# Add and GELU on one core: one DMA queue with late stores, adds on GpSimd, a sigmoid form through PSUM

## The chip, the core and the metric

The kernel runs on one core of one Trainium2 chip. The core has five engines that run side by side, each through its own list of instructions in order: TensorE (PE, not used here), VectorE (DVE), ScalarE (ACT), GpSimd (POOL) and SyncE (SP, which here only issues transfers). Sixteen DMA engines carry data between the chip's main memory (HBM) and the on-chip memory SBUF, which has 128 partitions. A second on-chip memory, PSUM, can be read and written by VectorE and ScalarE. The metric is the device time of one execution in microseconds (us); lower is better.

## The reference

Two float32 arrays of 1024 rows and 4096 columns are added, and the tanh form of GELU is taken of the sum, element by element:

```python
def reference(x, y):
    z = x + y
    return (0.5 * z * (1 + np.tanh(np.sqrt(2 / np.pi) * (z + 0.044715 * z ** 3)))).astype(np.float32)
```

Two arrays of 16.8 MB are read and one is written, 50.3 MB in all. Since 0.5 (1 + tanh u) is the sigmoid of 2u, the same function can be written z times sigmoid(2u).

## The kernel before

Each partition owns eight consecutive rows of the arrays, that is 32768 consecutive numbers in HBM. These columns are cut into 15 pieces of 2048 and a tail of 1024, 512, 256, 128 and 128. A piece of 2048 columns is 1 MiB per array: 128 runs of 8 KiB.

For every piece the kernel does eight things:

- two loads, issued by SP (L67 for x into a tile `a`, L68 for y into a tile `b`); six buffers of each;
- on VectorE, z = a + b (L75);
- on ScalarE, w = k3 z squared (the Square at L81, its factor folded into the scale);
- on VectorE, w = (w + k1) z (L90), the argument of tanh;
- on ScalarE, w = tanh(w) (L100), then w = 0.5 w + 0.5 (L105, whose bias is a one-column tile);
- on VectorE, w = z w (L116);
- one store, issued by GpSimd (L117), as soon as the product of the piece is there.

So VectorE has three instructions per piece and ScalarE three. The tiles z and w have five buffers each, all in SBUF. The loop at the end of the function emits the pieces in a software pipeline (loads of piece t beside the add of piece t - 1, and so on), and a scheduler in the tile framework sets the final order on each engine. SP carries loads only: a load of a piece waits until an earlier transfer has landed, and no more than eight loads are in flight. GpSimd carries stores only. The two queues share the sixteen DMA engines.

Of the kernel before, what the change touches and what calls it, by code (L numbers as in the profile page):

```python
# [1 line left out]

# [1 line left out]

# [4 lines left out]


@with_exitstack
def kernel(
    ctx: ExitStack,
    tc: tile.TileContext,
    x: bass.AP,
    y: bass.AP,
    out: bass.AP,
):
    nc = tc.nc  # L20
    P = nc.NUM_PARTITIONS
    fp32 = mybir.dt.float32

    N, D = x.shape
    assert N % P == 0
    rows_per_part = N // P

    k1 = math.sqrt(2.0 / math.pi)
    k3 = k1 * 0.044715
    sqrt_k3 = math.sqrt(k3)  # L30

    xv = x.rearrange("(p n) d -> p (n d)", p=P)
    yv = y.rearrange("(p n) d -> p (n d)", p=P)
    ov = out.rearrange("(p n) d -> p (n d)", p=P)

    total_free = rows_per_part * D
    FMAX = 2048

    tail = [1024, 512, 256, 128, 128]
    nbody = (total_free - sum(tail)) // FMAX  # L40
    assert sum(tail) + nbody * FMAX == total_free
    sizes = [FMAX] * nbody + tail
    offsets = []
    off = 0
    for F in sizes:
        offsets.append(off)
        off += F
    C = len(sizes)

    in_pool = ctx.enter_context(tc.tile_pool(name="inputs", bufs=6))  # L50
    chain_pool = ctx.enter_context(tc.tile_pool(name="chain", bufs=5))
    consts = ctx.enter_context(tc.tile_pool(name="consts", bufs=1))

    half = consts.tile([P, 1], fp32, tag="half")
    nc.vector.memset(half, 0.5)  # L55

    a_t: list = [None] * C
    b_t: list = [None] * C
    z_t: list = [None] * C
    w_t: list = [None] * C  # L60

    def do_load(c):
        F = sizes[c]
        sl = slice(offsets[c], offsets[c] + F)
        a = in_pool.tile([P, F], fp32, tag="a")
        b = in_pool.tile([P, F], fp32, tag="b")
        nc.sync.dma_start(out=a, in_=xv[:, sl])  # L67
        nc.sync.dma_start(out=b, in_=yv[:, sl])  # L68
        a_t[c] = a
        b_t[c] = b  # L70

    def do_add(c):
        F = sizes[c]
        z = chain_pool.tile([P, F], fp32, tag="z")
        nc.vector.tensor_add(out=z, in0=a_t[c], in1=b_t[c])  # L75
        z_t[c] = z

    def do_sq(c):
        F = sizes[c]
        w = chain_pool.tile([P, F], fp32, tag="w")  # L80
        nc.scalar.activation(  # L81
            out=w,
            in_=z_t[c],
            func=mybir.ActivationFunctionType.Square,
            scale=sqrt_k3,
        )
        w_t[c] = w

    def do_stt(c):
        nc.vector.scalar_tensor_tensor(  # L90
            out=w_t[c],
            in0=w_t[c],
            scalar=k1,
            in1=z_t[c],
            op0=mybir.AluOpType.add,
            op1=mybir.AluOpType.mult,
        )

    def do_ti(c):
        nc.scalar.activation(  # L100
            out=w_t[c],
            in_=w_t[c],
            func=mybir.ActivationFunctionType.Tanh,
        )
        nc.scalar.activation(  # L105
            out=w_t[c],
            in_=w_t[c],
            func=mybir.ActivationFunctionType.Identity,
            scale=0.5,
            bias=half,  # L110
        )

    def do_mul_store(c):
        F = sizes[c]
        sl = slice(offsets[c], offsets[c] + F)
        nc.vector.tensor_mul(out=w_t[c], in0=z_t[c], in1=w_t[c])  # L116
        nc.gpsimd.dma_start(out=ov[:, sl], in_=w_t[c])  # L117

    for t in range(C + 4):
        if 0 <= t < C:  # L120
            do_load(t)
        if 0 <= t - 3 < C:
            do_ti(t - 3)
        if 0 <= t - 1 < C:
            do_add(t - 1)
        if 0 <= t - 2 < C:
            do_stt(t - 2)
        if 0 <= t - 1 < C:
            do_sq(t - 1)
        if 0 <= t - 3 < C:  # L130
            do_mul_store(t - 3)


# [1 line left out]
_INS = ['x', 'y']  # L135
_OUTS = [((1024, 4096), 'float32')]


# [23 lines left out]
```

## Time and profile before

| what | value |
|---|---|
| time, median of 3 runs | 132.72 us (132.6 to 132.73) |
| span of the profiled execution, first to last instruction | 130.8 us |
| median less span | 1.9 us |
| VectorE busy | 107.8 us (82% of the span) |
| ScalarE busy | 96.0 us (73%) |
| GpSimd busy | 11.0 us (8%) |
| moved by the loads' queue (q1) and the stores' queue (q0) | 33.56 MB and 16.78 MB |
| mean rate over the span | 385 GB/s |

The profile comes from one execution; the runs of the time table are others. The profiled execution's own time is taken as its span and the 1.9 us that lie around it. The page gives busy times of engines, the traffic of the DMA engines in 40 equal slices of the span (3.27 us each), and the chain of waits that ended last. In the views by window, each row gives a stretch of the span, the busy time of the engines in it, and the DMA engines' rate. SPq and POOLq mark instructions that issue transfers.

### The profile page before, as it was taken

The numbers are of one execution on the slowest core, as the hardware profiler recorded it, in microseconds if no ns is written. First come the engines' busy times: TensorE is split into PE (matmuls) and PEld (weight loads), VectorE is DVE, ScalarE is ACT, GpSimd is POOL, SyncE is SP. The second block draws the span as 40 slices with busy tenths as digits, with TensorE's granted clock in tenths as the row PEclk, the third lists the DMA queues.
The fourth block names the chain that finished last, engine by engine and source line by source line (L and its number), as shares of the span: only waits on it lengthen the run. The fifth ranks groups of instructions, "written<-read, shape, count | busy, mean of one in ns | idle before, by whom it ended". The sixth has DMA issues, their size and how long they took to land.

```text
span 130.8 us, 306 instructions
## 1 busy us (share of the span) xinstructions
DVE 107.8 (82%) x61; ACT 96.0 (73%) x61; POOL 11.0 (8%) x24
## 2 busy tenths in 40 slices
DVE  0053949999999999988959899998969799999930
ACT  3005492899998989895975979885975959899850
POOL 0000002001000000101010100101010100110341
DMA  4999999999999999999999999999999999717690
GB/s 140 428 421 431 431 416 428 341 423 416 439 426 418 436 429 418 436 428 418 436 426 421 436 423 423 434 426 421 436 426 421 417 414 389 310 53 321 271 342 29
DMA packets 8258, 50.35 MB, mean 385 GB/s; under 512 B 960, under 2 KB 1728, under 8 KB 2496
## 3 DMA queue, kind: packets, MB, share of 16 engines
q1 hardware_dynamic: 5760, 33.56, 62.1%
q0 software_dynamic: 2496, 16.78, 30.9%
q14 instruction: 2, 0.02, 0.0%
HBM read 33.55 MB, written 16.78 MB: 385 GB/s over the span
## 4 chain that ended last, share of the span: by engine, by line
DMA 44%; issue 43%; POOL 5%; DVE 3%; POOLq 1%; SPq 0%; DVEq 0%
DMA b<-in_y_dram 44%; POOL out_dram L117 5%; DVE w L90 2%; DVE w L116 2%; POOLq L157 0%; SPq L67 0%; POOLq L117 0%; DVE z L75 0%; DVEq L75 0%
## 5 line engine op out<-in xcount | busy, mean ns | idle before, releaser
L75 DVE TENSOR_TENSOR z<-a,b 128x2048 f32<-128x2048 f32 (+4 forms) x20 | 37.2, 1862 | 13.1 <-DMA b<-in_y_dram 13.1
L81 ACT ACTIVATE w<-z 128x2048 f32<-128x2048 f32 (+4 forms) x20 | 31.3, 1563 | 22.5 <-DVE z L75 22.1
L116 DVE TENSOR_TENSOR w<-z,w 128x2048 f32<-128x2048 f32 (+4 forms) x20 | 37.2, 1860 | 3.0 <-ACT w L105 3.0
L90 DVE SCALAR_TENSOR_TENSOR w<-w,z 128x2048 f32<-128x2048 f32 (+4 forms) x20 | 37.1, 1859 | 2.4 <-ACT w L81 2.4
L100 ACT ACTIVATE w<-w 128x2048 f32<-128x2048 f32 (+4 forms) x20 | 31.3, 1566 | 7.0 <-DVE w L90 6.9
L105 ACT ACTIVATE w<-w,half 128x2048 f32<-128x2048 f32 (+4 forms) x20 | 33.2, 1659 | 0.6
L117 POOL DMA_DIRECT2D out_dram<-w x20 | 10.8, 541 | 116.6 <-DVE w L116 114.7
L81 ACT ACT_TABLE_LOAD x1 | 1.3, 1283 | 0.7 <-PEq L146 0.7
L55 DVE MEMSET half<- 128x1 f32 x1 | 0.1, 59 | 0.8 <-PEq L146 0.8
L146 POOL MEMSET const-float32-0.0<- 128x1 f32 x1 | 0.1, 98 | 0.2 <-issue 0.2
L146 POOL MEMSET const-bfloat16-1.0<- 128x1 bf16 x1 | 0.1, 101 | 0.0
L146 POOL MEMSET const-float32-1.0<- 128x1 f32 x1 | 0.1, 98 | 0.0
L146 POOL MEMSET const-uint8-127<- 128x1 uint8 x1 | 0.1, 98 | 0.0
## 6 DMA issues: line engine op xcount, KB each, us to landing
a<-in_x_dram SPq DMA_DIRECT2D x15, 1024.0 KB, 27.4
b<-in_y_dram SPq DMA_DIRECT2D x15, 1024.0 KB, 28.2
out_dram<-w POOLq DMA_DIRECT2D x15, 1024.0 KB, 9.1
a<-in_x_dram SPq DMA_DIRECT2D x1, 512.0 KB, 28.7
b<-in_y_dram SPq DMA_DIRECT2D x1, 512.0 KB, 26.3
out_dram<-w POOLq DMA_DIRECT2D x1, 512.0 KB, 3.8
a<-in_x_dram SPq DMA_DIRECT2D x1, 256.0 KB, 23.2
b<-in_y_dram SPq DMA_DIRECT2D x1, 256.0 KB, 21.4
```

The costliest lines, as they stand in the source:

```text
L55: nc.vector.memset(half, 0.5)
L75: nc.vector.tensor_add(out=z, in0=a_t[c], in1=b_t[c])
L81: nc.scalar.activation(out=w, in_=z_t[c], func=mybir.ActivationFunctionType.Square, scale=sqrt_k3,)
L90: nc.vector.scalar_tensor_tensor(out=w_t[c], in0=w_t[c], scalar=k1, in1=z_t[c], op0=mybir.AluOpType.add, op1=mybir.AluOpType.mult,)
L100: nc.scalar.activation(out=w_t[c], in_=w_t[c], func=mybir.ActivationFunctionType.Tanh,)
L105: nc.scalar.activation(out=w_t[c], in_=w_t[c], func=mybir.ActivationFunctionType.Identity, scale=0.5, bias=half,)
L116: nc.vector.tensor_mul(out=w_t[c], in0=z_t[c], in1=w_t[c])
L117: nc.gpsimd.dma_start(out=ov[:, sl], in_=w_t[c])
L146: nc = _bacc.Bacc("TRN2", target_bir_lowering=False, num_devices=1)
```

## The change

The kernel function is rewritten. What it computes is the same function in the sigmoid form, and:

- **Pieces.** A tile is now up to 4096 columns of a block of 128 rows: 1024, 1024, 2048, then six of 4096, then 2048, 1024, 512, 512. A transfer of a 4096-column tile is 2 MiB, contiguous in HBM. Compute goes in chunks of up to 1024 columns, 33 of them.
- **x stays.** Every x tile has its own place in SBUF. The sum z is written over x, the product over z, and the store reads from there. y has four buffers of 4096 columns.
- **One queue.** SP issues loads and stores. A store of a tile stands in SP's list where the loads are 8192 columns past the tile's end. Everything left is stored at the end.
- **GpSimd adds.** The add of chunks 2 to 30 (29 of 33) is done by GpSimd; VectorE does the first two and the last two.
- **Sigmoid form, PSUM.** The chunk's temporary w lies in PSUM (four buffers of 1024 columns). ScalarE does a Square and a Sigmoid, VectorE (w + c1) z and w z. The step 0.5 w + 0.5 is gone.
- **Order by hand.** Four lists (SP, GpSimd, ScalarE, VectorE) fix each engine's order. A one-column Sigmoid ahead of everything loads the function table.

The old function is shown whole above, so only the added lines stand here.

```diff
+    c1 = 2.0 * math.sqrt(2.0 / math.pi)
+    root = math.sqrt(c1 * 0.044715)
+    LEAD = 8192
+    CH = 1024
+    YB = 4
+    sizes = [1024, 1024, 2048] + [D] * (NB - 2) + [2048, 1024, 512, 512]
...
+    def hbm(ap, t):
+        n, o = divmod(starts[t], D)
+        assert o + sizes[t] <= D
+        return ap[n * P : (n + 1) * P, o : o + sizes[t]]
...
+    by_pool = set(range(2, C - 2))
+    xpool = ctx.enter_context(tc.tile_pool(name="xz", bufs=1))
+    ypool = ctx.enter_context(tc.tile_pool(name="y", bufs=YB))
+    ppool = ctx.enter_context(
+        tc.tile_pool(name="w", bufs=4, space=bass.MemoryType.PSUM)
+    )
+    def load_x(t):
+        xt[t] = xpool.tile([P, sizes[t]], fp32, tag=f"x{t}", name=f"x{t}")
+        nc.sync.dma_start(out=xt[t], in_=hbm(x, t))
...
+        nc.sync.dma_start(out=yt[t], in_=hbm(y, t))
+    def store(t):
+        nc.sync.dma_start(out=hbm(out, t), in_=xt[t])
...
+    def add(c):
+        t, o, f = chunks[c]
+        eng = nc.gpsimd if c in by_pool else nc.vector
+        eng.tensor_add(out=z(c), in0=z(c), in1=yt[t][:, o : o + f])
+    def sq(c):
+        f = chunks[c][2]
+        wt[c] = ppool.tile([P, CH], fp32, tag="w", name=f"w{c}")[:, :f]
+        nc.scalar.activation(out=wt[c], in_=z(c), func=act.Square, scale=root)
+    def stt(c):
+        nc.vector.scalar_tensor_tensor(
+            out=wt[c], in0=wt[c], scalar=c1, in1=z(c), op0=alu.add, op1=alu.mult
         )
+    def sig(c):
+        nc.scalar.activation(out=wt[c], in_=wt[c], func=act.Sigmoid)
+    def mul(c):
+        nc.vector.tensor_mul(out=z(c), in0=wt[c], in1=z(c))
+    sp, pool, dve, acts = [], [], [], []
+    s = 0
+    for t in range(T):
+        sp += [(load_x, t), (load_y, t)]
+        while s < T and starts[s] + sizes[s] + LEAD <= starts[t] + sizes[t]:
+            sp.append((store, s))
+            s += 1
+    sp += [(store, t) for t in range(s, T)]
...
+    for i in range(-3, C + 1):
+        if 0 <= i < C:
+            dve.append((stt, i))
+            acts.append((sig, i))
+        if 0 <= i - 1 < C:
+            dve.append((mul, i - 1))
+        if 0 <= i + 3 < C and i + 3 not in by_pool:
+            dve.append((add, i + 3))
+        if 0 <= i + 2 < C:
+            acts.append((sq, i + 2))
...
+        one = xpool.tile([P, 1], fp32, tag="one", name="one")
+        nc.vector.memset(one, 0.0)
+        nc.scalar.activation(out=one, in_=one, func=act.Sigmoid)
```

On SP, the list before is loads alone, x and y by turns (`a` and `b` are their tiles):

```order
L67 DMA a<-in_x_dram 128x2048
L68 DMA b<-in_y_dram 128x2048
L67 DMA a<-in_x_dram 128x2048
L68 DMA b<-in_y_dram 128x2048
L67 DMA a<-in_x_dram 128x2048
```

In the new program it stands as below behind the loads of the first three tiles. `x_69`, `x_73` and `x_76` are the first three x tiles, `x_79` and `x_83` the first two of 4096 columns, `y_...` the y tiles.

```order
L74 DMA x_79<-in_x_dram 128x4096
L81 DMA y_81<-in_y_dram 128x4096
L74 DMA x_83<-in_x_dram 128x4096
L81 DMA y_85<-in_y_dram 128x4096
L84 DMA out_dram<-x_69 128x1024
L84 DMA out_dram<-x_73 128x1024
L84 DMA out_dram<-x_76 128x2048
L74 DMA x_127<-in_x_dram 128x4096
L81 DMA y_129<-in_y_dram 128x4096
L84 DMA out_dram<-x_79 128x4096
L74 DMA x_156<-in_x_dram 128x4096
```

The first three stores stand behind the loads of 12 MiB, and from there every store of a full tile stands between the loads of the tile two places on and three places on; those later loads stand behind it.

The end of SP's list in the new program, from the last store that is followed by a load (`x_247`, `x_250` and `x_253` are the small last tiles):

```order
L84 DMA out_dram<-x_156 128x4096
L74 DMA x_243<-in_x_dram 128x2048
L81 DMA y_245<-in_y_dram 128x2048
...
L74 DMA x_253<-in_x_dram 128x512
L81 DMA y_245<-in_y_dram 128x512
L84 DMA out_dram<-x_185 128x4096
L84 DMA out_dram<-x_214 128x4096
L84 DMA out_dram<-x_243 128x2048
L84 DMA out_dram<-x_247 128x1024
L84 DMA out_dram<-x_250 128x512
L84 DMA out_dram<-x_253 128x512
```

Six stores, 6 MiB, now stand behind the last load; before, stores had a queue of their own on GpSimd.

On VectorE, the list before ends like this (L75 is the add, L90 the STT, L116 the product; the pieces shrink):

```order
L75 TENSOR_TENSOR z<-a,b 128x512
L90 SCALAR_TENSOR_TENSOR w<-w,z 128x1024
L75 TENSOR_TENSOR z<-a,b 128x256
L116 TENSOR_TENSOR w<-z,w 128x2048
L90 SCALAR_TENSOR_TENSOR w<-w,z 128x512
L116 TENSOR_TENSOR w<-z,w 128x1024
```

The new program's list at the border to tile `x_79`, and its end (`w_...` are the PSUM temporaries; STT is the SCALAR_TENSOR_TENSOR of the function `stt`, and the TENSOR_TENSOR at L109 is `mul`, at L93 `add`):

```order
L101 SCALAR_TENSOR_TENSOR w_117<-w_117,x_79 128x1024
L109 TENSOR_TENSOR x_76<-w_109,x_76 128x1024
...
L109 TENSOR_TENSOR x_214<-w_287,x_214 128x1024
L93 TENSOR_TENSOR x_250<-x_250,y_245 128x512
L101 SCALAR_TENSOR_TENSOR w_297<-w_297,x_243 128x1024
L109 TENSOR_TENSOR x_243<-w_292,x_243 128x1024
L93 TENSOR_TENSOR x_253<-x_253,y_245 128x512
L101 SCALAR_TENSOR_TENSOR w_303<-w_303,x_247 128x1024
L109 TENSOR_TENSOR x_243<-w_297,x_243 128x1024
L101 SCALAR_TENSOR_TENSOR w_308<-w_308,x_250 128x512
```

The last product of a tile stands behind the first STT of the next tile, and in the end the adds of the last two small tiles stand among the work of `x_243`.

More of the change, by code (lines that the diff above doesn't have):

```diff
@@ L22 @@
     fp32 = mybir.dt.float32
+    act = mybir.ActivationFunctionType
+    alu = mybir.AluOpType
     N, D = x.shape
     assert N % P == 0
[L26 to L85, printed above, removed]
-        )
[L87 to L131, printed above, removed]
+    NB = N // P
+    TOT = NB * D
+    c1 = 2.0 * math.sqrt(2.0 / math.pi)
+    root = math.sqrt(c1 * 0.044715)
+    LEAD = 8192
+    CH = 1024
@@ new lines @@
+    YB = 4
+    sizes = [1024, 1024, 2048] + [D] * (NB - 2) + [2048, 1024, 512, 512]
+    assert sum(sizes) == TOT
+    starts = [sum(sizes[:t]) for t in range(len(sizes))]
+    T = len(sizes)
+    def hbm(ap, t):
+        n, o = divmod(starts[t], D)
+        assert o + sizes[t] <= D
+        return ap[n * P : (n + 1) * P, o : o + sizes[t]]
+    chunks = []
+    for t in range(T):
+        o = 0
+        while o < sizes[t]:
+            f = min(CH, sizes[t] - o)
+            chunks.append((t, o, f))
+            o += f
@@ new lines @@
+    C = len(chunks)
+    last = {t: c for c, (t, _, _) in enumerate(chunks)}
+    by_pool = set(range(2, C - 2))
[4 more added lines that the diff above has]
+    )
+    xt, yb, yt, wt = {}, {}, {}, {}
+    def load_x(t):
+        xt[t] = xpool.tile([P, sizes[t]], fp32, tag=f"x{t}", name=f"x{t}")
+        nc.sync.dma_start(out=xt[t], in_=hbm(x, t))
@@ new lines @@
+    sp, pool, dve, acts = [], [], [], []
+    s = 0
+    for t in range(T):
+        sp += [(load_x, t), (load_y, t)]
[3 more added lines that the diff above has]
+    sp += [(store, t) for t in range(s, T)]
+    for c in range(C):
+        if c in by_pool:
+            pool.append((add, c))
+    for i in range(-3, C + 1):
[8 more added lines that the diff above has]
+            acts.append((sq, i + 2))
@@ new lines @@
+    needs = {
+        load_x: lambda t: [],
+        load_y: lambda t: [
+            (add, c)
+            for c, (i, _, _) in enumerate(chunks)
+            if starts[t] % D == 0 and starts[i] // D == starts[t] // D - YB
+        ],
+        add: lambda c: [(load_y, chunks[c][0]), (load_x, chunks[c][0])],
+        sq: lambda c: [(add, c)] + ([(mul, c - 4)] if c >= 4 else []),
+        stt: lambda c: [(sq, c)],
+        sig: lambda c: [(stt, c)],
+        mul: lambda c: [(sig, c)],
+        store: lambda t: [(mul, last[t])],
+    }
@@ new lines @@
+    queues = [sp, pool, acts, dve]
+    done = set()
+    with tc.manual_schedule():
+        one = xpool.tile([P, 1], fp32, tag="one", name="one")
+        nc.vector.memset(one, 0.0)
+        nc.scalar.activation(out=one, in_=one, func=act.Sigmoid)
+        while any(queues):
+            moved = False
+            for q in queues:
+                while q and all(n in done for n in needs[q[0][0]](q[0][1])):
+                    fn, arg = q.pop(0)
+                    fn(arg)
+                    done.add((fn, arg))
+                    moved = True
+                    if q is not sp:
+                        break
+            assert moved, [q[:1] for q in queues]
```

8 lines of the change are left out of this document (added).

## Prediction

> **What bounds the kernel now.** I read the head of the page first, then the rates by stretch of the span, then SP's own waits.
>
> ```profile
> span 130.8 us, 306 instructions
> DVE 107.8 (82%) x61; ACT 96.0 (73%) x61; POOL 11.0 (8%) x24
> ...
> DMA packets 8258, 50.35 MB, mean 385 GB/s; under 512 B 960, under 2 KB 1728, under 8 KB 2496
> ...
> q1 hardware_dynamic: 5760, 33.56, 62.1%
> q0 software_dynamic: 2496, 16.78, 30.9%
> ...
> GB/s 140 428 421 431 431 416 428 341 423 416 439 426 418 436 429 418 436 428 418 436 426 421 436 423 423 434 426 421 436 426 421 417 414 389 310 53 321 271 342 29
> ```
>
> No engine is full, and the two queues' packets took 93% of the DMA engines' span. The stretches say where the other 7% and the slow packets are (columns: stretch and length, busy time of DVE, ACT, POOL with counts, PE's clock, DMA share, GB/s):
>
> ```profile
> 0.00:3.30 3.30, 0.06 (x1) 1.28 (x1) 0.20 (x4) 1.00 0.45 141
> ...
> 6.50:21.00 14.50, 9.08 (x5) 7.62 (x4) 0.00 (x0) 1.00 1.02 427
> ...
> 23.00:27.00 4.00, 4.00 (x3) 3.47 (x2) 0.00 (x0) 1.00 1.02 365
> ...
> 40.00:100.00 60.00, 54.96 (x26) 47.88 (x26) 4.25 (x8) 1.00 1.01 428
> ...
> 118.00:120.00 2.00, 2.00 (x3) 2.00 (x4) 0.00 (x0) 1.00 1.04 426
> ...
> 110.00:129.00 19.00, 15.43 (x19) 14.71 (x19) 4.29 (x8) 1.00 0.64 249
> 129.00:130.80 1.80, 0.00 (x0) 0.00 (x0) 0.00 (x0) 1.00 0.00 0
> ```
>
> Loads alone (6.5 to 21) run at 427 GB/s, loads and stores from two queues (40 to 100) at 428, and one large store alone (118 to 120, of the 1 MiB store issued at 116.87) at 426. These three agree, so about 427 GB/s is what the DMA engines give whatever the direction, and they are saturated up to 110 us. The loss is at the end: 110 to 129 moves 249 x 19.0 = 4.73 MB, 11.1 us of work at 427, so 7.9 us are lost. There the loads are over and the stores trickle behind VectorE and ScalarE:
>
> ```profile
> 107.43 0.33 SPq L68 DMA_DIRECT2D b<-in_y_dram  x1
> ...
> 116.87 0.53 POOL L117 DMA_DIRECT2D out_dram<-w  x1 [5.01 <-DVE w L116]
> ...
> 127.34 0.54 POOL L117 DMA_DIRECT2D out_dram<-w  x1 [1.28 <-DVE w L116]
> ...
> out_dram<-w POOLq DMA_DIRECT2D x1, 512.0 KB, 3.8
> ```
>
> VectorE worked through 15.4 of those 19 us: it is late by its backlog. So the body is bound by DMA, the tail by compute, and at most the tail (7.9 us) and small change can be won.
>
> **The stream, step by step.** The change moves the same 50.35 MB. The start is the same: SP issues, nothing waits. I keep 0 to 3.3 us as measured: 141 x 3.3 = 0.465 MB. The other 49.88 MB at 427 GB/s take 116.8 us, so the last packet ends at 120.1 if the queue never runs dry. One MiB takes 2.456 us. The stretch at 23 to 27 us, when the first stores join, lost 4 x 62/427 = 0.6 us; the change has a first store too. Bounds 0 and 0.6; I take 0.6, since that row is the nearest. From the last packet to the end of the span lie 1.8 us (129.0 to 130.8). Sum: 3.3 + 116.8 + 0.6 + 1.8 = **122.5 us of span**, and with 1.9 us around it (132.72 less 130.8) **124.4 us**.
>
> Stores and loads in one queue: bounds are the three rates above, 426 to 428, and I take 427. Runs are now 16 KiB in most tiles. No row has that; the best slice of the page shows 439, so a gain to 436 all through would be 2.4 us (49.88/0.436 = 114.4). I take none.
>
> **Does the queue run dry?** Durations of chunks:
>
> ```profile
> L75 DVE TENSOR_TENSOR z<-a,b 128x1024 f32<-128x1024 f32 x1 | 1.2, 1218 | 0.0
> L90 DVE SCALAR_TENSOR_TENSOR w<-w,z 128x1024 f32<-128x1024 f32 x1 | 1.2, 1218 | 0.0
> L116 DVE TENSOR_TENSOR w<-z,w 128x1024 f32<-128x1024 f32 x1 | 1.2, 1219 | 0.0
> L75 DVE TENSOR_TENSOR z<-a,b 128x512 f32<-128x512 f32 x1 | 0.7, 686 | 0.0
> L81 ACT ACTIVATE w<-z 128x1024 f32<-128x1024 f32 x1 | 1.0, 1042 | 0.0
> L100 ACT ACTIVATE w<-w 128x1024 f32<-128x1024 f32 x1 | 1.0, 1040 | 0.0
> L105 ACT ACTIVATE w<-w,half 128x1024 f32<-128x1024 f32 x1 | 1.1, 1132 | 0.0
> ...
> L146 POOL MEMSET const-float32-0.0<- 128x1 f32 x1 | 0.1, 98 | 0.2 <-issue 0.2
> L55 DVE MEMSET half<- 128x1 f32 x1 | 0.1, 59 | 0.8 <-PEq L146 0.8
> ```
>
> A chunk of 1024 columns brings 1 MiB in and 0.5 MiB out: 3.68 us of DMA in the steady state.
>
> - *ScalarE* loses the 1.13 of L105: 1.04 + 1.04 = 2.1 us per chunk, 67 us in all. Hidden. Sigmoid is priced like the tanh row; the table load (1.28 us) ends before the first data, as before.
> - *VectorE* loses the add: 2 x 1.22 = 2.44 us per chunk, 33 chunks and four adds, 82 us. No row has a PSUM operand. Below: 1.14 (half of a 2048-column instruction of 2.29, no fixed cost). Above: 2.44, if reading and writing the same temporary took turns. I take 1.22: same instruction, shape and type. [...]
> - *GpSimd* has no add in the trace. Below: 1.22, VectorE's. Above: 3.65, three times that, if two reads and one write passed one after another. Its memset costs 98 ns against VectorE's 59, a ratio of 1.66, which makes 2.0 us; I take that, the only row that compares the two engines. 29 adds are 58 us, 2.0 of each 3.68. [...]
> - *SP* issues 39 transfers instead of 40, at 0.33 us (the L68 row), all under running transfers. The 20 issues on GpSimd go.
>
> *The stores' place.* A store waits for its tile's last product, and on VectorE that product stands behind the next tile's first STT, which needs that tile's loads, one GpSimd add (2.0) and one Square (1.04). So a tile's store can be issued 2.0 + 1.04 + 1.22 + 1.22 = 5.5 us after the *next* tile lands. In the queue there lie, between that landing and the store's turn, the previous store (2 MiB) and the next loads (4 MiB): 14.7 us. A store's first packets come about 1.0 us after its issue (116.87, and full rate by 118.0). Spare: 14.7 - 5.5 - 1.0 = 8.2 us per tile. At the start it is tightest for `x_76`: `x_79` has landed at 3.3 + (8.39 - 0.465)/0.427 = 21.9, so its store goes at 27.4; its turn comes when 12 MiB of loads and two stores of 0.5 MiB have passed, at 3.3 + (12.58 + 1.05 - 0.465)/0.427 = 34.1, less 1.0 for the issue. Spare 5.7. Loads behind a waiting store share its spare. A load of y that waits for GpSimd waits for adds of four tiles before. None of this shows.
>
> *The tail.* Counted back from 120.1: six stores (6 MiB) stand behind the last load, which ends at 105.4. `x_214` lands 12 MiB before the end, at 90.6. Its first STT starts at 90.6 + 2.0 + 1.04 = 93.7. From there VectorE runs 14 instructions of 1.22 and two adds of 0.69 to the last product of `x_243`: 112.2. That store's turn is 2 MiB before the end, 115.2, less 1.0 for the issue: 114.2. Spare 2.0 us; the last two tiles follow with 0.61 us of DMA each. Stall 0. It becomes late when a VectorE instruction costs over (114.2 - 93.7 - 1.4)/14 = 1.36 us, or a GpSimd add over 2.9 (90.6 + 7p + 3.5 > 114.2).
>
> **The rivals.**
>
> *A better stream.* 2 MiB transfers at 436 and no dip: 124.4 - 2.4 - 0.6 = 121.4. For: slices of 436 to 439; against: the mean of 428 where the queue was always full.
>
> *A late tail.* VectorE at 1.5 to 1.7 us with PSUM, or GpSimd near 3.3. At 1.6, the product of `x_243` comes at 93.7 + 22.4 + 1.4 = 117.5, 3.3 late: 127.7. Between 126 and 130. For: no row has PSUM. Against: the same engine pays 1.218 to 1.219 for three kinds of instruction.
>
> *GpSimd and VectorE shut each other out (slower).* If an add and a VectorE instruction cannot run together, a chunk costs 2 x 1.22 + 2.0 = 4.44 us, over the 3.68 from which it decides. The first GpSimd tile lands at 12.0 (4 MiB); 29 x 4.44 = 128.8; then Square, STT, Sigmoid, product (4.5), a last store (3.8) and 1.8: 150.9, with 1.9 **152.8 us**. GpSimd's own price of 4.0 would give 12.0 + 116 + 10.1 + 1.9 = 140. For: both work on SBUF, and GpSimd's adds stand nowhere in the trace. Against: GpSimd's issues beside a busy VectorE cost the same each time:
>
> ```profile
> L117 POOL DMA_DIRECT2D out_dram<-w x20: 531/532/673, 21.3 to 127.3; - x20
> ```
>
> [...]
>
> *Turning the queue (slower).* The new list changes direction 11 times. If every change empties the engines for the 1.0 us from issue to first packet, that costs 11 us: 135.4. It decides from (132.7 - 124.4)/11 = 0.75 us per change. For: before, each queue has one direction. Against: 428 GB/s with both directions in the engines at once.
>
> *No gain.* Stalls of 8 us from several sides: 132.4, for which nothing single speaks.
>
> **How the numbers follow.** Forecast 124.4 us, chance 0.68 with 122.6 to 126 as its own range; better stream 0.06; late tail 0.13; shut out 0.05; turning 0.05; no gain 0.03. A tenth of the chance lies slower and beyond 130; so the range is 121.6 to 129.5. About 0.2% is what the measurement can tell from no change: faster 0.87, same 0.03, slower 0.10.
>
> **What would show it.** Right: the rate stays near 427 to the last slice, no gap between 110 us and the end, DMA engines idle only for the first 2 and the last 2 us; GpSimd's adds near 2 us; SP's waits for VectorE end before the queue is empty. Wrong: a hole ahead of the stores of `x_214` or `x_243` (late tail), holes at each store (shut out), a dip at each change of direction (turning), or an add over 2.9 us.

## The result and the profile after

The changed kernel takes **127.19 us** (126.97 to 127.51, four runs) against 132.7 us: a ratio of 0.9587, 95% interval 0.9572 to 0.9601. The forecast was 124.4 us with a range of 121.6 to 129.5: faster, as foreseen, by 5.5 us instead of 8.3.

The head of the page after, with the rate in 40 slices and the only queue:

```profile
span 125.4 us, 301 instructions
DVE 79.1 (63%) x71; ACT 64.2 (51%) x68; POOL 67.4 (54%) x33
...
GB/s 106 255 410 429 462 418 439 429 429 418 401 430 397 434 366 376 428 439 429 434 439 423 428 423 444 423 449 418 418 418 421 415 421 400 433 439 434 324 398 161
...
q1 hardware_dynamic: 5616, 50.33, 97.0%
```

VectorE fell from 107.8 to 79.1 us, ScalarE from 96.0 to 64.2, and GpSimd now works for 67.4 us. The hole of before (53 GB/s in one slice near the end) is gone. The last two slices stay low, and two new low places stand at the start and in slices 13 to 16. The stretches (columns as in the prediction):

```profile
0.00:3.30 3.30, 0.06 (x1) 1.49 (x2) 0.20 (x4) 1.00 0.45 113
3.30:6.50 3.20, 0.00 (x0) 0.00 (x0) 0.00 (x0) 1.00 0.89 261
6.50:21.00 14.50, 8.44 (x8) 6.31 (x7) 4.64 (x2) 1.00 1.02 430
21.00:31.00 10.00, 4.86 (x5) 4.09 (x5) 6.17 (x3) 1.00 1.01 433
31.00:60.00 29.00, 21.34 (x19) 17.93 (x19) 21.32 (x10) 1.00 1.00 410
60.00:80.00 20.00, 13.02 (x12) 9.72 (x10) 9.55 (x5) 1.00 1.01 432
80.00:100.00 20.00, 10.81 (x10) 10.00 (x11) 14.22 (x7) 1.00 1.00 424
100.00:110.00 10.00, 9.46 (x9) 7.96 (x9) 9.46 (x5) 1.00 1.06 428
110.00:120.00 10.00, 10.00 (x11) 6.26 (x9) 1.81 (x1) 1.00 0.92 390
```

The kernel before had this in the second stretch:

```profile
3.30:6.50 3.20, 0.00 (x0) 0.00 (x0) 0.00 (x0) 1.00 1.01 425
```

Against 427 GB/s the start loses 3.2 x 166/427 = 1.2 us (and 0.2 before 3.3 us, against the 141 GB/s that the forecast kept), 31 to 60 us loses 29 x 17/427 = 1.2 us, 80 to 100 loses 0.1 and 110 to 120 loses 10 x 37/427 = 0.9 us; the stretches above 427 give back 0.5. The forecast had charged 0.6. This accounts for about 2.5 of the 2.9 us by which the span (125.4) exceeds the forecast one (122.5); the rest is the low rate of the last packets, 381 GB/s from 120 to 123.6 us.

The groups by shape give the prices that no row of before had (busy time in us and mean ns of one, then the engine's idle time before them and what ended it):

```profile
L93 POOL TENSOR_TENSOR x<-x,y 128x1024 f32<-128x1024 f32 x29 | 67.2, 2348 | 44.2 <-DMA y<-in_y_dram 44.2
L101 DVE SCALAR_TENSOR_TENSOR w<-w,x 128x1024 f32<-128x1024 f32 x31 | 38.1, 1231 | 33.3 <-ACT w L98 33.3
L109 DVE TENSOR_TENSOR x<-w,x 128x1024 f32<-128x1024 f32 x31 | 37.6, 1213 | 0.0
L98 ACT ACTIVATE w<-x 128x1024 f32<-128x1024 f32 x31 | 31.9, 1028 | 52.0 <-POOL x L93 44.0 <-DVE x L93 8.0
L106 ACT ACTIVATE w<-w 128x1024 f32<-128x1024 f32 x31 | 30.5, 983 | 2.1 <-DVE w L101 2.0
```

GpSimd's add takes 2.35 us (2.0 taken), VectorE with one operand in PSUM 1.21 to 1.23 (1.22 taken). GpSimd now waits for data for 44 us: it is ahead of the stream.

### The profile page after: what moved, and what is told of

It is laid out like the page before. It is cut to its first block, busy times and chain, and to the rows that moved or that the text cites. A ratio compares the mean times of both kernels' runs of the same rounds, so it can differ in the third digit from the quotient of the medians.

```text
span 125.4 us, 301 instructions
## 1 busy us (share of the span) xinstructions
DVE 79.1 (63%) x71; ACT 64.2 (51%) x68; POOL 67.4 (54%) x33
## 4 chain that ended last, share of the span: by engine, by line
DMA 63%; POOL 15%; DVE 11%; SPq 4%; ACT 2%; issue 2%; POOLq 0%
DMA y<-in_y_dram 63%; POOL x L93 15%; DVE x L109 5%; DVE w L101 5%; SPq L74 2%; ACT w L98 2%; SPq L81 1%; DVE x L93 1%; ACT w L106 0%; SPq L84 0%; POOLq L93 0%
## 5 line engine op out<-in xcount | busy, mean ns | idle before, releaser
L93 POOL TENSOR_TENSOR x<-x,y 128x1024 f32<-128x1024 f32 x29 | 67.2, 2348 | 44.2 <-DMA y<-in_y_dram 44.2
L101 DVE SCALAR_TENSOR_TENSOR w<-w,x 128x1024 f32<-128x1024 f32 (+1 forms) x33 | 39.5, 1198 | 33.3 <-ACT w L98 33.3
L98 ACT ACTIVATE w<-x 128x1024 f32<-128x1024 f32 (+1 forms) x33 | 33.1, 1002 | 52.0 <-POOL x L93 44.0
L109 DVE TENSOR_TENSOR x<-w,x 128x1024 f32<-128x1024 f32 (+1 forms) x33 | 39.0, 1181 | 0.1
L106 ACT ACTIVATE w<-w 128x1024 f32<-128x1024 f32 (+1 forms) x33 | 31.6, 958 | 3.5 <-DVE w L101 3.4
L93 DVE TENSOR_TENSOR x<-x,y 128x1024 f32<-128x1024 f32 (+1 forms) x4 | 4.9, 1231 | 7.9 <-DMA y<-in_y_dram 7.9
```

Source lines behind the costliest of these rows:

```text
L93: eng.tensor_add(out=z(c), in0=z(c), in1=yt[t][:, o : o + f])
L98: nc.scalar.activation(out=wt[c], in_=z(c), func=act.Square, scale=root)
L101: nc.vector.scalar_tensor_tensor(out=wt[c], in0=wt[c], scalar=c1, in1=z(c), op0=alu.add, op1=alu.mult)
L106: nc.scalar.activation(out=wt[c], in_=wt[c], func=act.Sigmoid)
L109: nc.vector.tensor_mul(out=z(c), in0=wt[c], in1=z(c))
```

## The experiments

**All stores last.** The queue changes direction once instead of 11 times.

```diff
-    LEAD = 8192
+    LEAD = 32768
```

> The new kernel with all stores behind the last load, so that the one queue changes direction once instead of 11 times. Theory A (changes of direction are free, the DMA engines give about 427 GB/s either way): the time stays within 1 us of the new kernel's 127.2 us. Rival B (each change costs some tenths of a us, which would explain the dips between 31 and 60 us): about 1.1 us less or more, 126 us, and the stretch 31 to 60 us runs at 427 GB/s and over.

125.85 us, ratio 0.9482 (0.9466 to 0.9499): 1.3 us faster than the changed kernel. The stretches:

```profile
3.30:6.50 3.20, 0.00 (x0) 0.00 (x0) 0.00 (x0) 1.00 0.88 275
...
31.00:60.00 29.00, 27.46 (x25) 22.94 (x25) 27.45 (x13) 1.00 1.01 430
60.00:80.00 20.00, 18.99 (x17) 15.98 (x17) 18.98 (x9) 1.00 1.00 418
...
110.00:120.00 10.00, 0.00 (x0) 0.00 (x0) 0.00 (x0) 1.00 0.99 423
```

The dip at 31 to 60 is gone (430 instead of 410, 1.4 us), and so is the low end (423 instead of 390), while 60 to 80, where the small late loads now pass, is lower (418 instead of 432, 0.65 us). Theory A missed its 1 us by 0.3, and the rival's time (126 us) came. But the rival's reason is not shown: in the changed kernel 60 to 80 us has several changes of direction and runs at 432.

**Larger first tiles.**

```diff
-    sizes = [1024, 1024, 2048] + [D] * (NB - 2) + [2048, 1024, 512, 512]
+    sizes = [2048, 2048] + [D] * (NB - 2) + [2048, 1024, 512, 512]
```

> The new kernel with first tiles of 2048 and 2048 columns instead of 1024, 1024 and 2048. Theory A (the slow first 6 us come from the first transfers, 512 KB in runs of 4 KiB): with 1 MiB in runs of 8 KiB the first 1 MiB lands near 5.6 us as in the kernel before, 1.3 to 1.8 us are won, 125.6 us. Rival B (the new layout in HBM, rows 16 KiB apart, makes the cold start slow): still about 260 GB/s between 3.3 and 6.5 us, 127.2 us.

126.28 us (ratio 0.9544, 0.9491 to 0.9597), 0.9 us faster by the medians; but three runs took 126.2 to 126.3 and one 127.74, and the interval overlaps the changed kernel's. So the gain in time is not certain; the rates show the start:

```profile
3.30:6.50 3.20, 0.00 (x0) 0.00 (x0) 0.00 (x0) 1.00 0.98 410
...
31.00:60.00 29.00, 21.59 (x20) 18.22 (x20) 20.12 (x9) 1.00 1.00 419
```

The start runs at 410 instead of 261 GB/s, which is worth 1.1 us of the 2.9.

**The old layout in HBM, same small first tiles.**

```diff
-        return ap[n * P : (n + 1) * P, o : o + sizes[t]]
+        flat = ap.rearrange("(p n) d -> p (n d)", p=P)
+        return flat[:, starts[t] : starts[t] + sizes[t]]
```

> The new kernel with the rows laid over the partitions as in the kernel before (each partition eight consecutive rows, runs 128 KiB apart instead of 16 KiB), all sizes kept. Theory A (small first transfers start slowly wherever they lie): again about 260 GB/s from 3.3 to 6.5 us. Rival B (the pitch of 16 KiB with runs of 4 KiB is what is slow): over 400 GB/s there and about 1.5 us less in all, 125.7 us.

126.05 us in one run. The row of the start:

```profile
3.30:6.50 3.20, 0.68 (x1) 0.00 (x0) 0.00 (x0) 1.00 1.04 424
```

So neither the size nor the run of 4 KiB alone was slow: the same transfers with runs 128 KiB apart started at 424 GB/s. What was slow at the start were 4 KiB runs 16 KiB apart (261 GB/s). They were not slow everywhere, though: in the changed kernel the third and fourth 512 KB transfers, of the same shape, landed (issue plus time to landing) 1.28 and 1.25 us after the one before them (at 8.65 and 9.90 us), near the 1.23 us that 427 GB/s gives. Only the first two were slow (5.04 and 7.37 us). Why pitch and cold start must come together is open.

**The temporary in SBUF instead of PSUM.**

```diff
-    YB = 4
+    YB = 3
...
-        tc.tile_pool(name="w", bufs=4, space=bass.MemoryType.PSUM)
+        tc.tile_pool(name="w", bufs=4)
```

> The new kernel with the temporary w in SBUF instead of PSUM (and three y buffers instead of four, for room). Every VectorE instruction then has two inputs in SBUF. Theory A (VectorE with two SBUF inputs and a GpSimd add shut each other out): 2.35 + 2 x 1.22 = 4.8 us per chunk, above the 3.68 us of DMA, so 15 + 29 x 4.8 + about 10 = 160 us or more, and some VectorE or GpSimd instructions last two to three times their own time. Rival B (they do not): the same 127 us and 1.2 and 2.35 us per instruction.

155.15 us in one run, 28 us slower than the changed kernel. Groups by shape, and the order of time in the body (start and length in us):

```profile
L93 POOL TENSOR_TENSOR x<-x,y 128x1024 f32<-128x1024 f32 x29 | 88.5, 3080 | 42.3 <-DMA y<-in_y_dram 42.3
L101 DVE SCALAR_TENSOR_TENSOR w<-w,x 128x1024 f32<-128x1024 f32 x31 | 66.5, 2144 | 11.5 <-ACT w L98 11.5
L109 DVE TENSOR_TENSOR x<-w,x 128x1024 f32<-128x1024 f32 x31 | 61.2, 1975 | 0.0
...
49.46 12.62 POOL L93 TENSOR_TENSOR x<-x,y 128x1024 f32<-128x1024 f32 x4 [0.51 <-DMA y<-in_y_dram]
49.95 3.37 DVE L109 TENSOR_TENSOR x<-w,x 128x1024 f32<-128x1024 f32 x1
...
53.24 3.35 DVE L101 SCALAR_TENSOR_TENSOR w<-w,x 128x1024 f32<-128x1024 f32 x1
```

While GpSimd adds, a VectorE instruction of 1.2 us lasts 3.4, and a GpSimd add mostly 3.3: nearly as long as both together, 3.4 us being 1.22 + 2.35 less 0.2. The missing fourth y buffer is not what costs here: SyncE's loads of y waited 0.9 us for GpSimd's adds in all, against 1.0 in the changed kernel. So the rival "shut out" shows in this run. It does not strike the changed kernel's products and STTs, whose w lies in PSUM: they take 1.21 and 1.23 us beside the adds. The changed kernel itself shows it once, at its end, where VectorE adds, with both inputs in SBUF, beside GpSimd: a 512-column add of 0.69 us lasts 1.80.

```profile
110.56 1.80 DVE L93 TENSOR_TENSOR x<-x,y 128x512 f32<-128x512 f32 x1
```

**All adds on VectorE.**

```diff
-    by_pool = set(range(2, C - 2))
+    by_pool = set()
```

> The new kernel with all adds on VectorE, GpSimd idle. VectorE then has 3 x 1.22 = 3.66 us per chunk against 3.68 us of DMA, and 121 us in all. If the move of the adds carries a part of the gain: VectorE is busy from 7.5 us to the end, stores come late at the end, and the time is 132 to 136 us. If not: 127 us as the new kernel.

135.48 us in one run, slower than the kernel before by 2%. Its stretches near the end:

```profile
110.00:114.00 4.00, 4.00 (x5) 2.55 (x4) 0.00 (x0) 1.00 0.99 421
114.00:118.00 4.00, 4.00 (x4) 2.54 (x3) 0.00 (x0) 1.00 0.18 78
118.00:122.00 4.00, 4.00 (x5) 1.95 (x3) 0.00 (x0) 1.00 0.15 66
```

The hole of the kernel before is back, though 6 MiB of stores stand behind the last load: VectorE is busy through it, late with the products that the stores wait for. Everything but the place of the adds is the changed kernel here. Part of the lateness may come from the order of VectorE's list, which was not varied: each add stands there three chunks ahead, and VectorE stood idle at adds for 19.4 us, waiting for loads.

**Stores in a second queue, not held back.** ScalarE issues them, two chunks after the tile's last product; SyncE has loads only.

```diff
-        nc.sync.dma_start(out=hbm(out, t), in_=xt[t])
+        nc.scalar.dma_start(out=hbm(out, t), in_=xt[t])
...
-            sp.append((store, s))
...
-    sp += [(store, t) for t in range(s, T)]
...
+        acts += [(store, t) for t in range(T) if last[t] + 2 == i or (i == C + 1 and last[t] + 2 > i)]
```

> The new kernel with the stores issued by ScalarE into a queue of its own, two chunks after the tile's last product, so that they run beside the loads instead of behind them. Theory A (the gain lies in the stores that are held back to cover the end): each store now takes its share of the engines at once, the loads end late, near 114 us, and after them stand only the last tiles' stores behind their compute: a hole of some us near the end, 130 us or more. Rival B (the one queue does not matter, the freed VectorE and ScalarE do): 127 us, no hole.

126.79 us (0.9561, 0.9538 to 0.9584), the same as the changed kernel within the intervals. Two stretches of it:

```profile
31.00:60.00 29.00, 23.69 (x21) 19.72 (x21) 21.46 (x10) 1.00 1.01 431
...
110.00:114.00 4.00, 4.00 (x4) 2.93 (x4) 0.71 (x1) 1.00 0.65 275
```

The hole that theory A foresaw is there (275 GB/s for 4 us, 1.4 us lost), but it is small, and the dip at 31 to 60 is gone in return. Theory A fell in its size: a second queue and prompt stores cost about what they save. One queue with stores held back is not what carries the gain.

**The old kernel with held stores alone.** Stores go into SyncE's queue behind the loads four pieces later; nine w buffers, five input buffers.

```diff
-    in_pool = ctx.enter_context(tc.tile_pool(name="inputs", bufs=6))
+    in_pool = ctx.enter_context(tc.tile_pool(name="inputs", bufs=5))
...
+    w_pool = ctx.enter_context(tc.tile_pool(name="w", bufs=9))
...
-        nc.gpsimd.dma_start(out=ov[:, sl], in_=w_t[c])
...
+        nc.sync.dma_start(out=ov[:, sl], in_=w_t[c])
...
+        if 0 <= t - 7 < C:
+            do_store(t - 7)
```

> The kernel before with one part of the change alone: its stores go into SyncE's queue, each behind the loads four pieces (8192 columns) later; nine w buffers and five input buffers instead of five and six, all else as it was. Theory A (the covered end carries the gain): the 7.9 us of hole at the end shrink to 2 or 3, 126 to 128 us; VectorE's 107.8 us still fit under the stream. Rival B (the compute was too slow for it, the moved adds and the dropped activation are needed as well): loads wait for buffers, holes in the body or at the end, 131 us or more.

140.46 us, ratio 1.0592 (1.0574 to 1.0609): slower. SyncE's own waits (us in all, how many, the longest), and two stretches:

```profile
SPq L68 <- DVE z L76: 23.0, 8, 7.1
...
SPq L119 <- DVE w L115: 13.2, 3, 8.9
...
80.00:100.00 20.00, 14.57 (x8) 14.38 (x9) 0.00 (x0) 1.00 1.01 425
...
110.00:114.00 4.00, 4.00 (x2) 1.89 (x1) 0.00 (x0) 1.00 0.25 107
```

Loads wait for input buffers (23 us) and stores for the product, in one list, and VectorE loses 5 us between 80 and 100 alone although it is the late one. With the old compute, the held stores are a loss. Two edits went together here (the queue and the buffers), so how much each costs is open; that held stores alone carry the gain is not borne out.

**The sigmoid form alone in the old kernel.** Square and Sigmoid, no L105; the factor k1 is doubled for it.

```diff
-    k1 = math.sqrt(2.0 / math.pi)
+    k1 = 2.0 * math.sqrt(2.0 / math.pi)
...
-            func=mybir.ActivationFunctionType.Tanh,
...
-            func=mybir.ActivationFunctionType.Identity,
-            scale=0.5,
-            bias=half,
+            func=mybir.ActivationFunctionType.Sigmoid,
```

> The kernel before with the sigmoid form alone: ScalarE does a Square and a Sigmoid per piece and no L105; all else as it was. Theory A (at the end VectorE's work is what is late; ScalarE's 33 us were hidden): 131 to 132.7 us, a gain under 1.5 us by the shorter chain of the last pieces. Rival B (ScalarE is what holds the last pieces up): 128 us or less.

132.75 us, ratio 1.0008 (0.9991 to 1.0025): no change, though ScalarE's busy time fell from 96.0 to 65.3 us. Its end is as before, with VectorE busy through it:

```profile
DVE 107.7 (82%) x61; ACT 65.3 (50%) x42; POOL 11.0 (8%) x24
...
110.00:129.00 19.00, 16.36 (x19) 9.15 (x12) 4.28 (x8) 1.00 0.65 255
```

In the old kernel ScalarE's work was hidden all along.

**Half the lead.**

```diff
-    LEAD = 8192
+    LEAD = 4096
```

> The new kernel with the stores 4096 columns behind the loads instead of 8192, nothing else changed. Theory A (the working of the prediction: a tile's store can go 5.5 us after the next tile has landed, and the loads behind it in SyncE's list wait with it): each store of a full tile leaves the queue empty for about 5.5 + 1.0 us, more with GpSimd at 2.35 us, six or seven times and at the end: 165 to 178 us, with holes in the DMA rate every 23 us. Rival B (SyncE runs far enough ahead): 127 to 130 us.

178.53 us in one run, half a us above theory A's range. SyncE in order of time, and its waits:

```profile
31.60 0.91 SPq L81 DMA_DIRECT2D y<-in_y_dram  x1
51.36 0.34 SPq L84 DMA_DIRECT2D out_dram<-x  x1
...
74.40 0.34 SPq L84 DMA_DIRECT2D out_dram<-x  x1
...
SPq L84 <- DVE x L109: 145.6, 13, 21.9
```

One tile passes every 23 us instead of 14.7, a loss of 8.3 us where theory A had 5.5 + 1.0: the next loads are issued only when the waiting store goes. With 8192 columns the spare of 8 us that the prediction worked out covers this wait.

**GpSimd takes the last adds too.**

```diff
-    by_pool = set(range(2, C - 2))
+    by_pool = set(range(2, C))
```

> The new kernel with the adds of the last two small tiles on GpSimd too, so that VectorE has no instruction with two SBUF inputs beside a GpSimd add at the end (one lasted 1.80 us there instead of 0.69). Theory A (the end is set by the queue, not by VectorE): no change beyond 0.3 us, 127.2 us. Rival B (VectorE's lateness at the end counts): 0.8 to 1.5 us faster, 126 us.

128.26 us, ratio 0.9681 (0.9632 to 0.9730): not faster, rather 1 us slower than the changed kernel, which neither theory had. VectorE ended 1.8 us earlier (119.4 instead of 121.2). Two stretches of this kernel:

```profile
110.00:120.00 10.00, 9.32 (x10) 6.99 (x9) 4.72 (x3) 1.00 0.99 424
...
122.00:124.00 2.00, 0.00 (x0) 0.00 (x0) 0.00 (x0) 1.00 0.41 160
```

110 to 120 us ran at 424 instead of 390 GB/s, yet the last packets came no sooner: from 122 to 124 us the DMA engines were busy for 41% only, and the last packets passed after 124 us, as in the changed kernel. So VectorE's end does not set the end, as theory A has it; why the last transfers thin out, and why the four runs are slower, is open.

**The best of it.** Stores last, first tiles of 2048, then seven of 4096.

```diff
-    LEAD = 8192
+    LEAD = 32768
-    sizes = [1024, 1024, 2048] + [D] * (NB - 2) + [2048, 1024, 512, 512]
+    sizes = [2048, 2048] + [D] * (NB - 1)
```

> The new kernel with all stores behind the last load, first tiles of 2048 and 2048 columns, and seven full tiles of 4096 instead of the shrinking end (16 MiB of stores cover the compute of the last tile). Theory A (the two losses found so far are separate: 1.3 us by changes of direction and small late transfers, 0.9 us by the small first transfers): 132.7 x 0.9482 less 0.9 to 1.3, 124.5 to 125.0 us, a rate of 425 GB/s and over in every stretch from 3.3 us to 120 us. Rival B (the same loss, counted twice): 125.8 us as with the stores last alone.

**123.76 us**, ratio 0.9333 (0.9319 to 0.9347): faster than both kernels, and 0.7 us better than theory A's best. The page's rates and two stretches:

```profile
GB/s 110 400 425 427 443 435 430 419 430 430 430 425 430 430 430 425 430 430 430 430 425 430 430 430 433 422 406 427 457 430 430 430 430 430 430 430 435 430 430 113
...
31.00:60.00 29.00, 27.45 (x25) 22.92 (x25) 27.42 (x13) 1.00 1.01 430
...
100.00:110.00 10.00, 0.00 (x0) 0.00 (x0) 0.00 (x0) 1.00 1.00 429
```

A flat 430 GB/s, one dip (406) at the one change of direction, and no compute in the last 20 us. This is the stream that the prediction summed: its forecast without the 0.6 of a dip was 123.8, and the last packets came near 120.1 us, as in its sum. Small errors cancel in that: the start was 0.3 us slower than in the sum, and much of the body ran a little above 427.

## Why the prediction was right, and where it was off

*The bound.* The body is the DMA stream and the end was compute that came too late: right. The sum for a stream that never runs dry (123.8 to 124.4 us) was reached by the last experiment, not by the change.

*The start.* The step "the start is the same" failed. The first transfers of 512 KB lie in runs of 4 KiB, 16 KiB apart, and ran at 261 GB/s where the old ones ran at 425: 1.2 to 1.4 us. With 1 MiB transfers, or with the old pitch, the start is back at 410 and 424.

*One rate for both directions.* Right on the whole (430 to 433 in undisturbed stretches), but the dip was mis-sized: 0.6 charged, 1.2 us lost between 31 and 60. It is absent with the stores last (430) or in a second queue (431), and 60 to 80 runs at 432 with the same alternation, so it is no fixed price per change of direction. The kernel before has such a dip when its first stores join, with two queues (365 GB/s from 23 to 27 us). The largest part of it in the changed kernel, about 0.7 us, lies at 46 to 48 us:

```profile
46.00:47.00 1.00, 1.00 (x2) 0.00 (x0) 0.00 (x0) 1.00 1.14 295
47.00:48.00 1.00, 0.31 (x1) 0.00 (x0) 0.00 (x0) 1.00 0.86 279
```

The DMA engines' share is 1.00 over these two us, so the queue had not run dry: the packets were slow. The cause is open.

*GpSimd.* 2.0 taken, 2.35 measured, hidden as said: the ratio of the two memsets (1.66) was too low for the adds (2.35 to 1.22, 1.93). That it runs beside VectorE at its own price rests here on PSUM, and 28 us hang on it: with w in SBUF the time was 155.15 us, near the 152.8 at which the prediction priced the rival "shut out". In the change only VectorE's four adds have two inputs in SBUF.

*VectorE.* 1.22 taken, 1.21 to 1.23 measured. No cost of PSUM as an operand shows in the duration: the same shapes in SBUF took 1.22 in the kernel before.

*The stores' place.* Right: 8192 columns leave spare, 4096 do not (178.5 us).

*The tail.* "Stall 0" was nearly right. The product of `x_243` was done at 117.5 instead of 112.2: `x_214` had landed at 94.9 instead of 90.6, and VectorE's 512-column add beside GpSimd lasted 1.80 us instead of 0.69, 1.1 us that the prediction had put at nothing. The store of `x_243` was issued at 117.52, while the 2 MiB of `x_214` still ran (they landed at 119.6), but the DMA engines were busy for 54% and 76% only:

```profile
117.00:118.00 1.00, 1.00 (x2) 0.92 (x2) 0.00 (x0) 1.00 0.54 229
118.00:119.00 1.00, 1.00 (x2) 0.58 (x1) 0.00 (x0) 1.00 0.76 320
```

These two us lost 0.7 us. It is a small case of the late tail that the prediction listed as a rival.

*What carries the gain.* The prediction credited the store order and the freed engines together. The runs separate them in part: with the adds on VectorE the new order is worse than the old kernel (135.5), held stores in the old kernel, with five input buffers, lose (140.5), a second queue with prompt stores gives the same (126.8), and ScalarE's relief gives nothing in the old kernel (132.75). So the gain needs VectorE's 2.44 instead of 3.66 us per chunk, and that needs the adds on GpSimd and the temporaries in PSUM (155.15 us with them in SBUF). Whether it is enough by itself is not shown: the new tile sizes, x kept in SBUF and the order by hand were in every run that gained. With all this in place, holding all stores back adds another 1.3 us.

## What to carry to other kernels

When the transfers are saturated (428 GB/s from 40 to 100 us in the kernel before) and only the end has a hole (249 from 110 to 129), look for the engine that is busy through the hole. Here the hole closed only with work taken from that engine, VectorE (107.8 to 79.1 us busy), while 31 us taken from ScalarE changed nothing (132.75 us). Before work is moved to GpSimd, look at where VectorE's operands lie: here the two ran side by side with one of VectorE's operands in PSUM (1.21 to 1.23 and 2.35 us), and shut each other out with both in SBUF (3.4 and 3.3 us). Loads first and all stores last made the end safe here (429 to 438 GB/s from 100 to 118 us in the last experiment), where SBUF could hold all the results.

## What the runs showed of the hardware

- VectorE instructions with two SBUF inputs and GpSimd adds at the same time lasted nearly as long as both together: 1.2 us became 3.4, and 2.35 became 3.3. With one of VectorE's inputs in PSUM both kept their own time (1.21 to 1.23, and 2.35).
- The first 512 KB transfers of the program, 4 KiB runs 16 KiB apart, moved 261 GB/s from 3.3 to 6.5 us; with runs 128 KiB apart 424. The third and fourth transfer, of the same shape, landed 1.28 and 1.25 us after the one before them.
- A ScalarE chunk of 1024 columns with PSUM as source and target took 983 ns (Sigmoid), from SBUF to PSUM 1028 (Square), within SBUF 1040 to 1042 (tanh and Square, the kernel before).
